# An attention stage: the scaling of the probabilities moved from VectorE to ScalarE

## The chip, the cores and the metric

The kernel runs on one core of a Trainium2 chip. Its engines work side by side, each through its own queue of instructions in order: TensorE (PE in the profile; its weight loads are PEld) multiplies matrices into PSUM, VectorE (DVE) and ScalarE (ACT) compute elementwise, GpSimd (POOL) and SyncE (SP) here mainly start DMAs. An instruction starts when its engine has come to it and the semaphores it waits for have been raised. The metric is the time of one execution on the device in microseconds (us), lower being better.

## What is computed

One decoder layer on 512 tokens with 2048 features: RMSNorm, a token mixer, a SwiGLU feed-forward part, and a last RMSNorm. The mixer is an attention of 16 heads (128 wide, 4 heads to a group of keys and values) with three branches, whose outputs are added with gates:

```python
gates = jax.nn.sigmoid(gl)                       # per token, branch and head
p_c = masked_softmax(s_c, mask_c)                # 31 compressed blocks of keys
o_c = jnp.einsum('bghtc,bcgd->btghd', p_c, vcc)
...                                              # o_s: selected blocks; o_w: sliding window
o = gates[0] * o_c + gates[1] * o_s + gates[2] * o_w
return o.reshape(Bsz, S, N_HEADS * DH) @ w_out
```

With 512 tokens all 8 blocks are selected and the window holds every earlier token, so the selected and the window branch are each a full causal attention, with keys and values of their own. A masked softmax divides exponentials by their row sum. The kernel therefore multiplies each row of exponentials by one factor, gate over sum, and then adds the branches up in one accumulation.

## The kernel before

All products are made in float32 from two parts: a high part rounded for TensorE, and the rest that the rounding leaves (names ending in h and l, or `whi`, `wlo`). Splitting a tile takes a copy on ScalarE (L97, L866, L293) and a subtraction on VectorE (L98, L870, L294), and a product takes three matmuls (L268 to L270).

The attention stage is a loop over heads `h` (L906), here called rounds 0 to 15, each of 12 steps `i`. In round `h` the values of head `h` are multiplied while head `h+1` gets its scores; both are cut into tiles of 128 tokens, `t` for queries (3 first, 0 last) and `kt` for keys. Between these pieces `pump` (L773) lets the stream `dense` put out the projections of later heads' queries, keys and values and, from round 12 on, part of the output projection: 20.8 us of TensorE work to a round by its own count. The order on every engine is the order of this Python code. A tile of probabilities goes this way:

- `scores(h+1, t)` at steps 2, 5, 8, 11 (t = 3, 2, 1, 0): score matmuls into the one PSUM tile `s`; VectorE adds the bias and takes the row maxima (`mx`, L828) for three regions: the 31 compressed columns (`cx`) and two branches of 128(t+1) columns each; ScalarE takes the exponentials and row sums (`sm`, L830) into `CX[t]` and `P[t]`.
- `finish(h+1, t)` at the next step (3, 6, 9, and step 0 of the following round for t = 0): VectorE takes the reciprocal of the sums (L835), multiplies it by the gates (L836), scales the three pieces (L842; the compressed one is copied three times into `P[t]`, 96 columns), and turns `P[t]` in blocks of 32x32 (L843); four DMAs on SyncE's queue store it to DRAM (L845).
- `fetch(t)` (L849) brings it back as `ptr`, so that keys lie on the partitions: tiles 3 and 2 at step 8, 1 at step 11, 0 at step 2 of the following round.
- `turn(h, b, kt)` at steps 0 to 8 splits it for branch `b` into `pth` (ScalarE, L866) and `ptl` (VectorE, L870), three and two buffers; `values` multiplies it two steps later into PSUM tile `o` (L884). `head_out` copies `o` to `stage` after step 11 (L890).

Within a step the order is `turn`, then `scores` or `finish`, then `values`, then `pump`. Ahead of round 0 the first head's four tiles go through `scores`, `finish` and `fetch` without rounds (L899 to L905). Weight tiles (`raw`, three buffers, loaded by GpSimd's queue in this stage) are split two granules ahead of their use.

Of the kernel before, what the change touches and what calls it, by code (L numbers as in the profile page):

```python
# [13 lines left out]
AF = mybir.ActivationFunctionType  # L14
OP = mybir.AluOpType
# [4 lines left out]
S, D, H, DH, G, HPG = 512, 2048, 16, 128, 4, 4  # L20
# [153 lines left out]
def nsa_block(ctx: ExitStack, tc: tile.TileContext, x, rel_bias, mix_g, ffn_g, fin_g, w_in, w_out,  # L174
              pos_k, w1k, w2k, pos_v, w1v, w2v, f_in, f_out, onehot, out):
    nc = tc.nc
    mm, act, dve, pool = nc.tensor.matmul, nc.scalar.activation, nc.vector, nc.gpsimd
# [28 lines left out]
    def tok(t):  # L206
        return slice(128 * t, 128 * (t + 1))
# [59 lines left out]
    def three(o, ah, al, bh, bl, start, stop):  # L267
        mm(o, ah, bh, start=start, stop=False, skip_group_check=True)  # L268
        mm(o, ah, bl, start=False, stop=False, skip_group_check=True)  # L269
        mm(o, al, bh, start=False, stop=stop, skip_group_check=True)  # L270
# [80 lines left out]
    with ExitStack() as st1:  # L351
# [11 lines left out]
        with ExitStack() as st0:  # L363
# [35 lines left out]
            def bank(shape):  # L399
                return ps1.tile(shape, F32, name=next(names))  # L400
# [49 lines left out]
            p = bank([128, 512])  # L450
            for i in range(N_WARM):
                nc.tensor.transpose(p[:, 128 * (i % 4):128 * (i % 4 + 1)], ident, ident)
            p = bank([128, KC])
# [29 lines left out]
            for q in range(4):  # L483
# [23 lines left out]
                if q == 3:  # L507
                    p = bank([128, S])
# [100 lines left out]
        for i in range(8):  # L609
            g = W.take()  # L610
            for t in range(NT):
# [4 lines left out]
                if i == 7:  # L616
                    act(ge[:, t], ps[t][:, 256:304].rearrange("p (n h) -> p n h", n=3), AF.Exp,
                        scale=yneg[:, t:t + 1])
                    v_out(ps[t][:, :256], t, VV[0][0][:, t], VV[0][1][:, t])
            if i == 1:  # L620
                p = ps1.tile([128, 128], F32, name="tr")
# [27 lines left out]
        p = ps1.tile([96, G, 128], F32, name="tr")  # L649
# [8 lines left out]
    with ExitStack() as st2:  # L658
# [3 lines left out]
        runs = [32 * (2 * t + 3) for t in range(NT)]  # L662
        P = [ap_.tile([128, 4, runs[t]], F32, name=f"p{t}", bufs=1) for t in range(NT)]
        CX = [ap_.tile([128, 32], F32, name=f"cx{t}", bufs=1) for t in range(NT)]
# [108 lines left out]
        def pump(h, step):  # L773
            at = h + (step + 4) / STEPS
            goal = 20800 * min(at, 13) + 22500 * max(at - 13, 0)
            while done["ns"] < goal:
                c = next(stream, "end")
                if c == "end":
                    return
                done["ns"] += c or 0  # L780

        def drain_to(n):
            while done["n"] < n:
                c = next(stream, "end")
                if c == "end":
                    return
                done["ns"] += c or 0

        def needed(h):

            return 4 * ((h - 2) // 4) + (1 if h % 4 > 1 else 3) if h > 1 else 0

        TB, HS = {}, {}
        sc = ps2.tile([128, 3, 512], F32, name="s", bufs=1).rearrange("p a c -> p (a c)")

        def load_bias(h):
            if h < H:
                TB[h] = ap_.tile([128, S], F32, name="tb")
                (nc.sync if h else pool).dma_start(TB[h], bass.AP(tensor=d_u.tensor, offset=d_u.offset + h * UL + 127,
                                                 ap=[[H * UL - 1, 128], [1, S]]))  # L800

        def branch(t, b):

            return P[t][:, :, 32 * (t + 1) * b:32 * (t + 1) * (b + 1)]

        def scores(h, t):
            g, n = h // HPG, 128 * (t + 1)
            (qh, ql), (kh, kl) = Q[h], KK[g % 2]
            if t == NT - 1:
                HS[h] = dict(  # L810
                    mx=ap_.tile([128, NT, 3], F32, name="mx"), sm=ap_.tile([128, NT, 3], F32, name="sm"))
            s = HS[h]
            at = 224 + (512 if t == 1 else 0)
            cuts = [0, 288] + [c for c in (800, 1056) if c <= 32 + 2 * n]
            if cuts[-1] < 32 + 2 * n:
                cuts.append(32 + 2 * n)
            for c0, c1 in zip(cuts, cuts[1:]):
                three(sc[:, at + c0:at + c1], qh[:, tok(t)], ql[:, tok(t)], kh[:, c0:c1], kl[:, c0:c1], True, True)
            c = CX[t][:, :NCMP]
            regions = [(c, c, c, sc[:, at:at + NCMP], biasc[:, h, 24 - 8 * t:24 - 8 * t + NCMP])]  # L820
            bt = TB[h][:, S - n:].rearrange("p (n s) -> p n s", s=128)
            sw = sc[:, at + 32:at + 32 + 2 * n].rearrange("p (n b s) -> p b n s", b=2, s=128)
            for b in range(2):
                u = ap_.tile([128, S], F32, name="u")[:, :n]
                regions.append((u.rearrange("p (n s) -> p n s", s=128), u.rearrange("p (n j s) -> p j n s", j=4, s=32),
                                branch(t, b).rearrange("p j (n s) -> p j n s", s=32), sw[:, b], bt))
            for i, (u, v, p, ps, bias) in enumerate(regions):
                dve.tensor_tensor_reduce(out=u, in0=ps, in1=bias, op0=OP.add, op1=OP.min, scale=-1.0,  # L828
                                         scalar=1e38, accum_out=s["mx"][:, t, i:i + 1])
                act(p, v, AF.Exp, bias=s["mx"][:, t, i:i + 1], scale=-1.0, accum_out=s["sm"][:, t, i:i + 1])  # L830
            s[t] = [c] + [branch(t, b) for b in range(2)]

        def finish(h, t):
            r = HS[h]["sm"][:, t]
            dve.reciprocal(r, r)  # L835
            dve.tensor_mul(r, r, gates[:, t, h])  # L836
            for i, p in enumerate(HS[h].pop(t)):
                o = p
                if not i:
                    o = P[t][:, :3, runs[t] - 32:]  # L840
                    p = CX[t].unsqueeze(1).to_broadcast([128, 3, 32])
                dve.tensor_scalar(o, p, r[:, i:i + 1], None, op0=OP.mult)  # L842
            dve.transpose(P[t], P[t])  # L843
            for i in range(4):
                nc.sync.dma_start(d_p[t][:, :, i].rearrange("j a r -> a j r"), P[t][32 * i:32 * (i + 1)])  # L845

        def fetch(t, queue=nc.sync):

            queue.dma_start(PT[:, :, PT_STEP * t:PT_STEP * t + runs[t]], d_p[t].rearrange("j a i r -> (j a) i r"))  # L849
# [6 lines left out]
        def turn(h, b, kt):  # L856
            n = S - 128 * kt
            th = ap_.tile([128, 512], F32R, name="pth", bufs=3)
            tl = ap_.tile([128, 512], F32R, name="ptl") if b >= 0 else th
            rows = 128 if b >= 0 else 96  # L860
            if b < 0:
                src = arrived(rows, 64, 0, PT_STEP + 64)
            else:
                src = arrived(rows, PT_STEP * kt + 32 * (kt + 1) * b + 32 * kt, kt, PT_STEP + 32 * b)
            th4, tl4 = (x[:rows, :n].rearrange("p (t i s) -> p t i s", i=4, s=32) for x in (th, tl))
            act(th4, src, AF.Copy)  # L866
            if b < 0:
                dve.tensor_tensor(th4[32:64], src[32:64], th4[32:64].bitcast(F32), op=OP.subtract)
            else:
                dve.tensor_tensor(tl4, src, th4.bitcast(F32), op=OP.subtract)  # L870
            HS[h]["t", b, kt] = th[:rows, :n], tl[:rows, :n]
# [27 lines left out]
        for i in range(4):  # L899
            scores(0, 3 - i)  # L900
            if i > 1:
                fetch(5 - i, pool)
            if i:
                finish(0, 4 - i)
            pump(-1, min(9 + i, 11.7))  # L905
        for h in range(H):  # L906
            seq = [(b, kt) for kt in (3, 2, 1, 0) for b in (0, 1)] + [(-1, 0)]
            for i in range(STEPS):
                if i == 4:
                    load_bias(h + 2)  # L910
                if i == 2:
                    fetch(0, nc.sync if h else pool)
                if i < 9:
                    turn(h, *seq[i])
                if i == 8 and h + 1 < H:
                    fetch(3)
                    fetch(2)
                if i == 11 and h + 1 < H:
                    fetch(1)
                if i == 0:  # L920
                    if not h:
                        fetch(1, pool)
                    finish(h, 0)
                if h + 1 < H:
                    if i == 2:
                        drain_to(needed(h + 1))
                    if i % 3 == 2:
                        scores(h + 1, 3 - i // 3)
                    elif i % 3 == 0 and i:
                        finish(h + 1, 4 - i // 3)  # L930
                if 2 <= i < 10 or i == 11:
                    if i == 2 and h % HPG == 0:
                        drain_to(h)
                    values(h, *seq[min(i - 2, 8)])
                    if i == 11:
                        head_out(h)
                pump(h, i)
# [563 lines left out]
    c = slice(1536, 2048)  # L1501
# [46 lines left out]
```

## Time and profile before

| what | value |
|---|---|
| median of three timed runs | 2126.79 us (2126.36 to 2128.25) |
| profiled execution, first to last instruction (span) | 2124.1 us |
| busy: TensorE, VectorE, ScalarE, GpSimd | 2100.1, 1634.4, 932.7, 125.8 us |
| attention stage in the trace | about 200 to 697 us |
| mean granted clock of TensorE | 0.996 |

The page gives no other time for the profiled execution than its span; what lies ahead of the first and behind the last instruction is in the timed runs only, whose median is 2.7 us longer. A timeline row gives the start and the length in us, the engine, the line, the instruction, what it writes and reads with the shape, a count, and in brackets how long the engine had been idle and what ended that. A row of the groups gives the count, then busy us and mean ns of one, then idle us ahead of them and what ended it. A row of the waits gives who waited for whom: us in total, times, the longest. A row of the stretches gives for each engine busy us and, as x, instructions, then TensorE's granted clock, the DMA share and GB/s.

### The profile page before, as it was taken

The numbers are of one execution on the slowest core, as the hardware profiler recorded it, in microseconds if no ns is written. First come the engines' busy times: TensorE is split into PE (matmuls) and PEld (weight loads), VectorE is DVE, ScalarE is ACT, GpSimd is POOL, SyncE is SP. The second block draws the span as 40 slices with busy tenths as digits, with TensorE's granted clock in tenths as the row PEclk, the third lists the DMA queues.
The fourth block names the chain that finished last, engine by engine and source line by source line (L and its number), as shares of the span: only waits on it lengthen the run. The fifth ranks groups of instructions, "written<-read, shape, count | busy, mean of one in ns | idle before, by whom it ended". The sixth has DMA issues, their size and how long they took to land.

```text
span 2124.1 us, 37169 instructions
## 1 busy us (share of the span) xinstructions
PE 2100.1 (99%) x14693; PEld 1948.4 (92%) x14693; DVE 1634.4 (77%) x2671; ACT 932.7 (44%) x1448; POOL 125.8 (6%) x206
## 2 busy tenths in 40 slices
PE   9999999999999999999999999999999999999998
PEld 7898788888989889999999999999999888999996
DVE  5565777877786366898888888888888777877785
ACT  5344455455554334444334343443434444444344
POOL 1000111111111000000000000000000000001000
PEclk9999999999999999999999999999999999999999
DMA  7555666676676643344344333433333776878894
GB/s 230 173 157 151 193 192 201 183 199 189 194 236 199 246 141 109 126 135 128 120 130 130 120 128 122 130 126 124 122 124 124 272 273 214 303 269 311 308 335 144
DMA packets 273227, 388.08 MB, mean 183 GB/s; under 512 B 34235, under 2 KB 205819, under 8 KB 272412
## 3 DMA queue, kind: packets, MB, share of 16 engines
q1 hardware_dynamic: 248252, 279.71, 41.7%
q0 software_dynamic: 22896, 102.31, 14.0%
q10 hardware_dynamic: 1904, 3.68, 0.5%
q8 instruction: 115, 1.88, 0.4%
q14 instruction: 60, 0.49, 0.1%
HBM read 320.52 MB, written 70.36 MB: 184 GB/s over the span
## 4 chain that ended last, share of the span: by engine, by line
PE 69%; DVE 0%; DMA 0%; ACT 0%; issue 0%; ACTq 0%
PE f L269 19%; PE f L268 19%; PE f L270 19%; PE proj L268 2%; PE proj L269 2%; PE proj L270 2%; PE pp L268 1%; PE pp L270 1%; PE pp L269 1%; PE po L269 1%; PE po L268 1%; PE po L270 1%; PE pp L246 0%; DMA acc<-d_a 0%; PE o L269 0%; PE o L270 0%
## 5 line engine op out<-in xcount | busy, mean ns | idle before, releaser
L98 DVE TENSOR_TENSOR wlo<-raw,whi 128x1024 fp32r<-128x1024 f32 (+1 forms) x225 | 269.4, 1199 | 117.6 <-ACT whi L97 117.3
L97 ACT ACTIVATE whi<-raw 128x1024 fp32r<-128x1024 f32 (+1 forms) x225 | 233.3, 1040 | 221.6 <-DVE raw L1038 122.9
L1038 DVE TENSOR_TENSOR tlo<-tt,thi 128x1536 fp32r<-128x1536 f32 (+2 forms) x135 | 197.1, 1460 | 111.0 <-ACT thi L1143 86.7
L269 PE MATMUL f<-hn_l,whi 128*128 128x256 f32 x984 | 271.6, 276 | 0.0
L270 PE MATMUL f<-hn_h,wlo 128*128 128x256 f32 x984 | 271.6, 276 | 0.0
L268 PE MATMUL f<-hn_h,whi 128*128 128x256 f32 x984 | 271.6, 276 | 0.0
L1138 ACT ACTIVATE whi<-raw 128x1024 fp32r<-128x1024 f32 x123 | 126.1, 1057 | 293.6 <-DVE raw L1038 290.2
L268 PE MATMUL proj<-hn_h,whi 128*128 128x512 f32 x512 | 204.8, 400 | 0.7 <-ACT hn_h L410 0.7
L269 PE MATMUL proj<-hn_l,whi 128*128 128x512 f32 x512 | 201.0, 393 | 0.3 <-DVE hn_l L411 0.3
L270 PE MATMUL proj<-hn_h,wlo 128*128 128x512 f32 x512 | 200.9, 392 | 0.0
L269 PEld LDWEIGHTS f<-hn_l,whi 128*128 128x128 f32 x984 | 184.7, 188 | 0.0
L268 PEld LDWEIGHTS f<-hn_h,whi 128*128 128x128 f32 x984 | 184.7, 188 | 0.0
L270 PEld LDWEIGHTS f<-hn_h,wlo 128*128 128x128 f32 x984 | 184.7, 188 | 0.0
L1143 ACT ACTIVATE thi<-tt 128x1536 fp32r<-128x1536 f32 x82 | 121.9, 1486 | 82.3 <-PE f L269 70.6
L270 PE MATMUL proj<-whi,hn_l 128*128 128x256 f32 (+2 forms) x496 | 146.1, 295 | 2.9 <-DVE hn_l L731 2.9
L1038 DVE TENSOR_TENSOR wlo<-raw,whi 128x1024 fp32r<-128x1024 f32 x123 | 147.0, 1223 | 1.1 <-ACT whi L1138 1.1
L268 PE MATMUL proj<-whi,hn_h 128*128 128x256 f32 (+2 forms) x496 | 146.5, 295 | 0.8 <-ACT hn_h L730 0.8
L269 PE MATMUL proj<-wlo,hn_h 128*128 128x256 f32 (+2 forms) x496 | 145.5, 293 | 0.0
L270 PE MATMUL f<-whi,tlo 128*128 128x512 f32 x320 | 124.9, 390 | 0.2 <-DVE tlo L1038 0.2
L269 PE MATMUL f<-wlo,thi 128*128 128x512 f32 x320 | 124.9, 390 | 0.0
L268 PE MATMUL f<-whi,thi 128*128 128x512 f32 x320 | 124.7, 390 | 0.0
L270 PEld LDWEIGHTS proj<-hn_h,wlo 128*128 128x128 f32 x512 | 96.7, 189 | 21.7 <-DVE wlo L98 0.2
(329 smaller groups left out, 6104.3 us busy)
## 6 DMA issues: line engine op xcount, KB each, us to landing
raw<-in_ffn_w_in SPq DMA_DIRECT2D x135, 512.0 KB, 3.6
raw<-in_ffn_w_out SPq DMA_DIRECT2D x88, 512.0 KB, 5.8
rawx<-in_ffn_w_in SPq DMA_DIRECT2D x41, 512.0 KB, 4.8
rawx<-d_a SPq DMA_DIRECT2D x31, 512.0 KB, 5.1
ah<-d_s POOLq DMA_DIRECT2D x16, 896.0 KB, 7.3
al<-d_s POOLq DMA_DIRECT2D x16, 896.0 KB, 9.4
raw<-in_nsa_w_in POOLq DMA_DIRECT2D x24, 512.0 KB, 4.7
raw<-in_nsa_w_in SPq DMA_DIRECT2D x23, 512.0 KB, 5.3
```

Source lines behind the costliest of these rows:

```text
L97: self.nc.scalar.activation(hi[:, :n], src, AF.Copy)
L98: self.nc.vector.tensor_tensor(lo[:, :n], src, hi[:, :n].bitcast(F32), op=OP.subtract)
L268: mm(o, ah, bh, start=start, stop=False, skip_group_check=True)
L269: mm(o, ah, bl, start=False, stop=False, skip_group_check=True)
L270: mm(o, al, bh, start=False, stop=stop, skip_group_check=True)
L1038: dve.tensor_tensor(o, a, b, op=OP.subtract)
L1138: act(h, r, AF.Copy)
L1143: act(h, ttf, AF.Copy)
```

## The change

`finish` becomes two functions. `weigh` makes the factors on VectorE as before and does the three multiplications on ScalarE, the two branches first, then the compressed columns; `send` turns the tile and stores it. In a step `weigh` now stands ahead of `turn`, `send` where `finish` stood. `scores` no longer keeps a list of pieces. From here on line numbers behind L838 are one higher.

```diff
-            s[t] = [c] + [branch(t, b) for b in range(2)]
-
-        def finish(h, t):
+
+        def weigh(h, t):
+
             r = HS[h]["sm"][:, t]
             dve.reciprocal(r, r)
             dve.tensor_mul(r, r, gates[:, t, h])
-            for i, p in enumerate(HS[h].pop(t)):
-                o = p
-                if not i:
-                    o = P[t][:, :3, runs[t] - 32:]
-                    p = CX[t].unsqueeze(1).to_broadcast([128, 3, 32])
-                dve.tensor_scalar(o, p, r[:, i:i + 1], None, op0=OP.mult)
+            for b in range(2):
+                p = branch(t, b)
+                act(p, p, AF.Copy, scale=r[:, b + 1:b + 2])
+            c = CX[t].unsqueeze(1).to_broadcast([128, 3, 32])
+            act(P[t][:, :3, runs[t] - 32:], c, AF.Copy, scale=r[:, :1])
+
+        def send(h, t):
             dve.transpose(P[t], P[t])
...
             if i:
-                finish(0, 4 - i)
+                weigh(0, 4 - i)
+                send(0, 4 - i)
...
+                if not i:
+                    weigh(h, 0)
+                elif i % 3 == 0 and h + 1 < H:
+                    weigh(h + 1, 4 - i // 3)
                 if i < 9:
                     turn(h, *seq[i])
...
-                    finish(h, 0)
+                    send(h, 0)
...
-                        finish(h + 1, 4 - i // 3)
+                        send(h + 1, 4 - i // 3)
```

What that does to the queues: the names `p_1857`, `p_1856`, `p_1855`, `p_1854` are `P[3]` to `P[0]`, and `cx_1861` to `cx_1858` are `CX[3]` to `CX[0]`. On ScalarE, from the end of one round (`stage`) to step 3 of the next, before:

```order
L890 ACTIVATE stage<-o 128x512
L866 ACTIVATE pth<-ptr 128x128
L97 ACTIVATE whi<-raw 128x1024
L866 ACTIVATE pth<-ptr 128x128
L866 ACTIVATE pth<-ptr 128x256
L830 ACTIVATE cx_1861,sm<-cx_1861,mx 128x31
L830 ACTIVATE p_1857,sm<-u,mx 128x4x128 x2
L866 ACTIVATE pth<-ptr 128x256
L97 ACTIVATE whi<-raw 128x1024
```

and now:

```order
L891 ACTIVATE stage<-o 128x512
L839 ACTIVATE p_1854<-p_1854,sm 128x4x32 x2
L841 ACTIVATE p_1854<-cx_1858,sm 128x3x32
L867 ACTIVATE pth<-ptr 128x128
L97 ACTIVATE whi<-raw 128x1024
L867 ACTIVATE pth<-ptr 128x128
L867 ACTIVATE pth<-ptr 128x256
L830 ACTIVATE cx_1861,sm<-cx_1861,mx 128x31
L830 ACTIVATE p_1857,sm<-u,mx 128x4x128 x2
L839 ACTIVATE p_1857<-p_1857,sm 128x4x128 x2
L841 ACTIVATE p_1857<-cx_1861,sm 128x3x32
L867 ACTIVATE pth<-ptr 128x256
```

The three multiplications of tile 0 now stand ahead of step 0's split and weight split, and those of tile 3 between step 2's exponentials and step 3's split. On VectorE at step 3, between the maxima of step 2 and those of step 5:

```order
-L870 TENSOR_TENSOR ptl<-ptr,pth 128x256
-L835 RECIPROCAL sm<-sm 128x3
-L836 TENSOR_TENSOR sm<-sm,gates 128x3
-L842 TENSOR_SCALAR p_1857<-cx_1861,sm 128x3x32
-L842 TENSOR_SCALAR p_1857<-p_1857,sm 128x4x128 x2
-L843 STREAM_TRANSPOSE p_1857<-p_1857 128x1152
-L98 TENSOR_TENSOR wlo<-raw,whi 128x1024
-L870 TENSOR_TENSOR ptl<-ptr,pth 128x384 x2
+L835 RECIPROCAL sm<-sm 128x3
+L836 TENSOR_TENSOR sm<-sm,gates 128x3
+L871 TENSOR_TENSOR ptl<-ptr,pth 128x256
+L844 STREAM_TRANSPOSE p_1857<-p_1857 128x1152
```

The two small operations on the factors come ahead of the split's rest (`ptl`) instead of behind it, and the multiplications are gone from between them and the transpose. At step 9 there is no `turn`, and VectorE goes from the factors straight to the transpose and then to step 11's maxima:

```order
 L835 RECIPROCAL sm<-sm 128x3
 L836 TENSOR_TENSOR sm<-sm,gates 128x3
-L842 TENSOR_SCALAR p_1855<-cx_1859,sm 128x3x32
-L842 TENSOR_SCALAR p_1855<-p_1855,sm 128x4x64 x2
-L843 STREAM_TRANSPOSE p_1855<-p_1855 128x640
+L844 STREAM_TRANSPOSE p_1855<-p_1855 128x640
 L828 ISA cx_1858,mx<-s,biasc 128x31
```

Only the multiplications left this queue there. TensorE's and SyncE's rows stand in the same order as before.

## Prediction

> **What bounds the kernel now.** I read the page's engine table first, then the stretches of the attention stage, then who waits for whom there, then the timeline of one head.
>
> ```profile
> PE 2100.1 (99%) x14693; PEld 1948.4 (92%) x14693; DVE 1634.4 (77%) x2671; ACT 932.7 (44%) x1448; POOL 125.8 (6%) x206
> ```
>
> ```profile
> core 0: us, PE busy (x) PEld busy (x) DVE busy (x) ACT busy (x) POOL busy (x), PEclk, DMA share, GB/s
> 200.00:245.00 45.00, 40.58 (x185) 33.62 (x184) 33.64 (x96) 20.11 (x55) 7.53 (x10) 0.92 0.61 170
> 245.00:700.00 455.00, 449.71 (x2735) 401.46 (x2734) 345.88 (x947) 235.44 (x612) 62.52 (x84) 1.00 0.69 200
> ```
>
> TensorE is busy for 99% of the span, and in the stage that the change touches (200 to 700 us) it is idle for 4.4 + 5.3 us. So hardly anything is left to win. What counts is what could make TensorE wait, and that shows in the waits of the other two engines in the same stage (total us, times, longest):
>
> ```profile
> ACT cx L830 <- DVE mx L828: 158.7, 64, 4.1
> DVE ptl L870 <- ACT pth L866: 63.3, 44, 2.9
> DVE cx L828 <- PE s L270: 2.1, 2, 1.6
> ```
>
> VectorE waits 63.3 us for ScalarE's split of the fetched probabilities, ScalarE waits 158.7 us for VectorE's row maxima, and VectorE waits for TensorE's scores only twice. So the two run as one chain, handing work to and fro, and that chain does not wait for TensorE: it is late against it all the time. How late, the timeline shows in head 6's round, first VectorE, then TensorE:
>
> ```profile
> 424.87 0.08 DVE L828 DVE_READ_ACCUMULATOR2_ANT mx<- 128x1 f32 x1
> ```
>
> ```profile
> 424.69 0.28 PE L269 MATMUL proj<-wlo,hn_h 128*128 128x256 f32 x1
> 424.81 0.28 PE L270 MATMUL proj<-whi,hn_l 128*128 128x256 f32 x1
> 425.01 0.40 PE L268 MATMUL s<-k1h,qh 128*128 128x288 f32 x1
> ```
>
> The score matmul of step 11 overwrites PSUM that VectorE has read until 424.95, and it starts at 425.01, where the rhythm of the matmuls ahead (0.12 us apart) would have had it at 424.93. So in this round TensorE arrives just when the chain lets it: the chain's round is as long as TensorE's, and the slack is gone. Whatever lengthens the chain from here on lengthens the stage; whatever shortens it gains almost nothing.
>
> **The change, part by part.** Off VectorE go 192 multiplications; onto ScalarE come 192. Rows of the groups kept apart by shape (mean ns of one):
>
> ```profile
> L842 DVE TENSOR_SCALAR p<-cx,sm 128x96 f32<-128x96 f32 x64 | 18.4, 288 | 2.5
> L842 DVE TENSOR_SCALAR p<-p,sm 128x512 f32<-128x512 f32 x32 | 14.2, 487 | 0.0
> L842 DVE TENSOR_SCALAR p<-p,sm 128x384 f32<-128x384 f32 x32 | 11.7, 409 | 0.0
> L842 DVE TENSOR_SCALAR p<-p,sm 128x256 f32<-128x256 f32 x32 | 9.8, 347 | 0.0
> L830 ACT ACTIVATE p<-u,mx 128x512 f32<-128x512 f32 x32 | 22.9, 716 | 3.3 <-DVE mx L828 3.0 <-ACT cx L830 0.2
> L830 ACT ACTIVATE p<-u,mx 128x384 f32<-128x384 f32 x32 | 19.5, 610 | 1.1
> L830 ACT ACTIVATE p<-u,mx 128x256 f32<-128x256 f32 x32 | 16.0, 502 | 0.0
> L830 ACT ACTIVATE p<-u,mx 128x128 f32<-128x128 f32 x32 | 12.4, 387 | 0.0
> L830 ACT ACTIVATE cx<-cx,mx 128x31 f32<-128x31 f32 x64 | 20.6, 321 | 158.7 <-DVE mx L828 158.7
> L866 ACT ACTIVATE pth<-ptr 128x512 fp32r<-128x512 f32 x32 | 19.5, 616 | 0.7 <-DMA ptr<-d_p 0.7
> ```
>
> ScalarE's multiplication is not in this trace. The nearest row is the exponential, which also takes a per-row operand from SBUF: 716, 610, 502, 387 ns. The lower end is the split without such an operand (616 ns for 512, so 0.1 less each). The 96-column copy lies between 321 (31 columns) and 387 (128): an estimate of 360. I take the exponential's row, because its operands are of the same kind. Following instructions overlap by about 0.1 us (below: 0.71 long, the next starts 0.61 later), so they advance by 0.61, 0.51, 0.40, 0.29 and 0.27; the upper end is no overlap.
>
> The Trainium skill (Perfetto Trace Analysis, Optimizing Scalar/DVE Operations) says that VectorE is faster where a 2x mode is available, and that moving work to ScalarE may make sense where VectorE is saturated. The trace agrees with the first (487 against 716 ns); on the second VectorE is busy 0.76 of the stage, so by that rule the move would win nothing, and the sum below says that it costs.
>
> The sum hangs on the handover. Step 3 of the round, VectorE and ScalarE:
>
> ```profile
> 405.93 0.08 DVE L828 DVE_READ_ACCUMULATOR2_ANT mx<- 128x1 f32 x1
> 407.30 0.42 DVE L870 TENSOR_TENSOR ptl<-ptr,pth 128x256 fp32r<-128x256 f32 x1 [1.28 <-ACT pth L866]
> 407.64 0.17 DVE L835 RECIPROCAL sm<-sm 128x3 f32<-128x3 f32 x1
> 408.04 0.29 DVE L842 TENSOR_SCALAR p<-cx,sm 128x96 f32<-128x96 f32 x1
> 408.24 0.87 DVE L842 TENSOR_SCALAR p<-p,sm 128x512 f32<-128x512 f32 x2
> 409.14 1.38 DVE L843 STREAM_TRANSPOSE p<-p 128x1152 f32<-128x1152 f32 x1
> ```
>
> ```profile
> 406.16 0.71 ACT L830 ACTIVATE p<-u,mx 128x512 f32<-128x512 f32 x1
> 406.77 0.19 ACT L830 ACTIVATION_READ_ACCUMULATOR p<-u,mx 128x1 f32 x1
> 406.86 0.40 ACT L866 ACTIVATE pth<-ptr 128x256 fp32r<-128x256 f32 x1
> ```
>
> Now: the split on ScalarE starts at 406.86, VectorE takes its rest at 407.30, then reciprocal and product (0.40), three multiplications (1.10, to 409.14), transpose. Afterwards the split stands behind the three multiplications, and these behind the factors, which need the last row sum (406.96). So ahead of the split come 0.10 (to 406.96), 0.04 to VectorE (407.26 to 407.30 is such a handover), 0.36 for the two small operations, 0.05 back, and 2 x 0.61 + 0.27 = 1.49 on ScalarE: 2.04. Behind it 0.40 + 1.10 = 1.50 fall away. Net **+0.54 us**. Nothing hides it: VectorE's next instructions (the split's rest, the transpose, the next weight split) are queued in order behind it, and it would wait there anyway.
>
> Step 6 (384 columns) alike: 2 x 0.51 + 0.27 + 0.55 = 1.84 ahead, and behind it 0.40 + 0.95 less (the multiplications 0.29 + 2 x 0.41, less 0.16, as 0.29 + 2 x 0.49 took 1.10 in step 3): **+0.49**. Step 9 (256) has no split in between: 2 x 0.40 + 0.36 + two handovers of 0.04 = 1.24 in place of 0.29 + 2 x 0.35 - 0.16 = 0.83: **+0.41**. In step 0 something covers it:
>
> ```profile
> 400.33 0.58 ACT L890 ACTIVATE stage<-o 128x512 f32<-128x512 f32 x1
> 401.00 1.05 ACT L97 ACTIVATE whi<-raw 128x1024 fp32r<-128x1024 f32 x1
> ```
>
> ```profile
> 402.96 1.18 DVE L98 TENSOR_TENSOR wlo<-raw,whi 128x1024 fp32r<-128x1024 f32 x1
> ```
>
> The three small multiplications (2 x 0.29 + 0.27 = 0.85, and some 0.06 of waiting for the factors, an estimate from the handovers of step 3) put the weight split's end from 402.05 to 402.96, and VectorE gets to that split's rest at 402.96 today, having done its own multiplications: **+0.05**. Without this cover it would be 0.9. Together the chain's round grows by 0.54 + 0.49 + 0.41 + 0.05 = **1.5 us**. Bounds: 0.1 us less in each of the nine multiplications of steps 3, 6 and 9 (no cost for the operand) gives 0.6, and 0.1 more (no overlap) gives 2.4.
>
> The start, before any round, is a run of such handovers (ScalarE, VectorE, TensorE):
>
> ```profile
> 209.04 0.19 ACT L830 ACTIVATION_READ_ACCUMULATOR p<-u,mx 128x1 f32 x1
> ```
>
> ```profile
> 209.72 1.38 DVE L843 STREAM_TRANSPOSE p<-p 128x1152 f32<-128x1152 f32 x1
> ```
>
> ```profile
> 220.92 0.45 PE L268 MATMUL o<-pth,v0h 128*128 128x128 f32 x1 [2.80 <-issue]
> ```
>
> The first transpose must now wait for ScalarE's exponentials of the second tile (to 209.23) and 1.49 of multiplications: 210.76 instead of 209.72, +1.0. The second tile adds 0.9 more in the same way, and its way through DRAM brings that to the chain: **+1.9** (0.9 to 2.8 by the same bounds).
>
> The new first half issues no DMA; the transpose's four stores and the fetches keep their places in SyncE's queue and move with the chain. GpSimd's weight loads wait for VectorE's weight splits and move with it too; two granules are held ready, so TensorE does not meet that. TensorE's own order is unchanged.
>
> How long does this last? Rounds 0 to 11 and the first half of round 12; after that the weight work thins out and TensorE is no longer met. At the meeting point of round 12 (VectorE, then TensorE):
>
> ```profile
> 607.12 0.08 DVE L828 DVE_READ_ACCUMULATOR2_ANT mx<- 128x1 f32 x1
> ```
>
> ```profile
> 607.80 0.29 PE L268 MATMUL s<-k1h,qh 128*128 128x288 f32 x1
> ```
>
> Slack there is 607.80 - 607.20 = 0.6. So: 1.9 + 12 x 1.5 + 1.0 (steps 3 and 6) - 0.6 = **+20.3 us**. Bounds: 0.9 + 12 x 0.6 + 0.4 - 0.6 = 8, and 2.8 + 12 x 2.4 + 1.6 - 0.6 = 32.6. The span of 2124.1 would be 2144.4. The median of the runs, 2126.79, lies 2.7 above the profiled span, and I leave that as it is: **2147 us**, from 2135 to 2159.
>
> **The rivals.** *Hidden* (8%): TensorE stays the bound and VectorE's spare time swallows the handovers: 2127. For it speaks TensorE's 99%, against it the 0.06 us of slack at 425.01 and that VectorE waits for ScalarE, not for TensorE. [...]
>
> *Faster* (5%): what limits the chain is VectorE's own work, and ScalarE's multiplications fit into its idle time, as if the 1.28 us of waiting took them in. Then a round of the chain loses some 3.5 us (1.10 + 0.95 + 0.83 and the small tile's), TensorE never waits in the rounds, and at most the 5.3 us of idle time between 245 and 700 come back: 2121.5. It would need the multiplications to run beside the split instead of ahead of it; the order on ScalarE says ahead.
>
> *Much slower* (7%): TensorE's new waits also drop its clock.
>
> ```profile
> 218.00:221.00 3.00, 0.20 (x3) 0.11 (x1) 0.15 (x1) 0.49 (x2) 2.27 (x3) 0.91 1.01 303
> 221.00:227.00 6.00, 6.00 (x17) 5.01 (x18) 3.56 (x15) 2.29 (x9) 0.76 (x1) 0.50 0.76 237
> ```
>
> After a wait of 2.80 us the granted clock was 0.50 for 6 us, so about 3 us of work were lost. Twelve times that on top: 2147 + 36 = 2183. It decides from waits of nearly 3 us in one piece; I expect some 1.5 per round. The Trainium skill (TensorE: Matmul & The Clock Gate, What's actually happening) halves the clock after an idle window of about 3.4 us; this trace agrees with the half, and shows it after 2.8.
>
> **How the numbers follow.** The forecast with its bounds has 80%, so the range is theirs, 2135 to 2159. Two kernels can be told apart here by about 0.2%, 4.3 us. The forecast and *much slower* lie above that: slower 87%. *Hidden* is the same, 8%. *Faster* 5%.
>
> **What would show it.** In the changed kernel's profile the ScalarE multiplications should have means of about 716, 610, 502 and 387 ns, and 360 for the copies; VectorE should wait for ScalarE's scaled tiles ahead of its transposes or split rests; TensorE's score matmul of step 11 should wait for the maxima in most rounds, and a round from score to score should last about 31.4 us. I am wrong if TensorE's idle time between 200 and 700 us stays near 10 us, and in the size if the scaling comes out nearer to 616 than to 716 ns.

## The result, and the profile after

| | median | lowest to highest | profiled span |
|---|---|---|---|
| before | 2126.74 us | 2126.36 to 2128.25 | 2124.1 us |
| after | 2151.22 us | 2150.24 to 2154.0 | 2148.8 us |

The changed kernel is slower, by 24.5 us going by the two medians. The ratio of the runs is 1.0122 (95%: 1.011 to 1.0135), which is clear of 1 and would be 25.9 us. The forecast was 20.3 us more, 2147 us, with a range of 2135 to 2159. Below, a difference in us of a timed kernel is its ratio's share of the kernel before that ran beside it (2125.8 and 2125.5 us in the experiments).

The page's engine table of the changed kernel:

```profile
PE 2114.3 (98%) x14693; PEld 1948.9 (91%) x14693; DVE 1580.4 (74%) x2479; ACT 1012.4 (47%) x1640; POOL 125.8 (6%) x206
```

VectorE has 54 us of work less, ScalarE 80 us more, and neither has become a full engine. TensorE's busy time grew by 14.2 us with the same 14693 matmuls, so the rise is best read as waiting that is shown as longer matmuls (the 16 matmuls 128x512 of `ptl` with `v1h` have a mean of 438 ns where they had 410). The weight loads' busy time, 1948.9 against 1948.4 us, shows that the work is the same. The Trainium skill (Perfetto Trace Analysis, Identifying the Most-Contended Engine) says that the busy share of the matmuls is not a good measure of how close TensorE is to its peak, and names the busy share of the weight loads among what to use instead; this trace agrees, the first rose by 14.2 us while the kernel became slower, the second by 0.5.

The stretches of the attention stage, which now ends some 25 us later:

```profile
core 0: us, PE busy (x) PEld busy (x) DVE busy (x) ACT busy (x) POOL busy (x), PEclk, DMA share, GB/s
200.00:245.00 45.00, 38.10 (x170) 30.77 (x169) 24.11 (x69) 25.00 (x68) 6.73 (x9) 0.92 0.55 150
245.00:720.00 475.00, 460.13 (x2723) 399.74 (x2721) 297.61 (x776) 306.40 (x783) 62.51 (x84) 1.00 0.67 190
```

TensorE is idle for 6.9 + 14.9 us where it had been idle for 4.4 + 5.3. The granted clock is 0.92 and 1.00, as before. Who waits for whom there (200 to 722 us; total us, times, longest):

```profile
ACT cx L830 <- DVE mx L828: 97.6, 64, 2.4
DVE ptl L871 <- ACT pth L867: 88.4, 49, 4.6
DVE sm L835 <- ACT p L830: 39.6, 44, 1.0
ACT p L839 <- DVE sm L836: 37.1, 48, 1.8
DVE p L844 <- ACT p L841: 25.2, 18, 2.2
```

The last two are new: ScalarE waits 48 times for the factors, VectorE waits 18 times for scaled tiles ahead of the transpose. VectorE's wait for ScalarE's split grew from 63.3 to 88.4 us, and its wait for the row sums, ahead of the factors, from 2.5 us (3 times) to 39.6. These two and the wait ahead of the transpose together grew by 87 us. What reaches TensorE is seen best at its weight loads, which show more of it than the matmuls (22.3 us against 8.1 in the change, for VectorE's split rests). Before (200 to 697 us), then after:

```profile
PEld s L268 <- DVE mx L828: 4.0, 7, 1.3
PEld o L269 <- DVE ptl L870: 3.0, 5, 1.0
```

```profile
PEld o L269 <- DVE ptl L871: 22.3, 43, 1.5
PEld s L268 <- DVE mx L828: 9.7, 14, 2.2
```

These two waits together are 25.0 us longer. Most of it is met not at the score matmul, as I had expected, but at the matmuls that use VectorE's rest of the split. In one round of the changed kernel (weight loads, in brackets the wait):

```profile
393.46 0.19 PEld L269 LDWEIGHTS o<-ptl,v1h 128*128 128x128 f32 x1 [0.76 <-DVE ptl L871]
401.73 0.19 PEld L269 LDWEIGHTS o<-ptl,v1h 128*128 128x128 f32 x1 [0.41 <-DVE ptl L871]
406.84 0.19 PEld L268 LDWEIGHTS s<-k1h,qh 128*128 128x128 f32 x1 [0.70 <-DVE mx L828]
416.68 0.19 PEld L269 LDWEIGHTS o<-ptl,v1h 128*128 128x128 f32 x1 [0.40 <-DVE ptl L871]
```

So TensorE is held four times in this round, 2.3 us in all, three times by split rests. The same four places recur in the other steady rounds, with waits of 0.15 to 0.76 us; the scores of step 11 start 0.05 to 0.06 us behind the maxima in each of rounds 0 to 11, and between 300 and 600 us their weight loads wait 0.31 to 0.72 us.

**The terms of the sum.** The start of VectorE's first row-maximum instruction (`cx<-s`) of each tile marks the chain's round: tile 3 at step 2, then tiles 2, 1, 0 and the next round's tile 3. Before, then after:

```profile
374.72 0.19 DVE L828 CUSTOM_DVE_ANT_0 cx<-s,biasc 128x31 f32<-128x31 f32 x1
382.62 0.18 DVE L828 CUSTOM_DVE_ANT_0 cx<-s,biasc 128x31 f32<-128x31 f32 x1
394.19 0.19 DVE L828 CUSTOM_DVE_ANT_0 cx<-s,biasc 128x31 f32<-128x31 f32 x1
399.04 0.15 DVE L828 CUSTOM_DVE_ANT_0 cx<-s,biasc 128x31 f32<-128x31 f32 x1
404.60 0.18 DVE L828 CUSTOM_DVE_ANT_0 cx<-s,biasc 128x31 f32<-128x31 f32 x1
```

```profile
385.32 0.18 DVE L828 CUSTOM_DVE_ANT_0 cx<-s,biasc 128x31 f32<-128x31 f32 x1
393.79 0.18 DVE L828 CUSTOM_DVE_ANT_0 cx<-s,biasc 128x31 f32<-128x31 f32 x1
405.90 0.19 DVE L828 CUSTOM_DVE_ANT_0 cx<-s,biasc 128x31 f32<-128x31 f32 x1
411.17 0.15 DVE L828 CUSTOM_DVE_ANT_0 cx<-s,biasc 128x31 f32<-128x31 f32 x1
416.88 0.18 DVE L828 CUSTOM_DVE_ANT_0 cx<-s,biasc 128x31 f32<-128x31 f32 x1
```

The four intervals hold the handovers of steps 3, 6, 9 and 0:

| interval with | before | after | longer by | forecast |
|---|---|---|---|---|
| step 3 | 7.90 | 8.47 | 0.57 | 0.54 |
| step 6 | 11.57 | 12.11 | 0.54 | 0.49 |
| step 9 | 4.85 | 5.27 | 0.42 | 0.41 |
| step 0 | 5.56 | 5.71 | 0.15 | 0.05 |
| round | 29.88 | 31.56 | 1.68 | 1.5 |

Step 3 of the changed kernel a round later, VectorE and then ScalarE, shows where these come from:

```profile
419.27 0.18 DVE L835 RECIPROCAL sm<-sm 128x3 f32<-128x3 f32 x1 [0.98 <-ACT p L830]
419.48 0.16 DVE L836 TENSOR_TENSOR sm<-sm,gates 128x3 f32<-128x3 f32 x1
421.68 0.43 DVE L871 TENSOR_TENSOR ptl<-ptr,pth 128x256 fp32r<-128x256 f32 x1 [2.04 <-ACT pth L867]
422.02 1.37 DVE L844 STREAM_TRANSPOSE p<-p 128x1152 f32<-128x1152 f32 x1
```

```profile
419.05 0.19 ACT L830 ACTIVATION_READ_ACCUMULATOR p<-u,mx 128x1 f32 x1
419.74 1.34 ACT L839 ACTIVATE p<-p,sm 128x512 f32<-128x512 f32 x2 [0.50 <-DVE sm L836]
420.98 0.36 ACT L841 ACTIVATE p<-cx,sm 128x96 f32<-128x96 f32 x1
421.25 0.40 ACT L867 ACTIVATE pth<-ptr 128x256 fp32r<-128x256 f32 x1
```

The row sum is there at 419.24, VectorE takes it at 419.27 (0.03 us), has the factors at 419.64, ScalarE starts on them at 419.74 (0.10 us), needs 1.51 us to the split at 421.25, and VectorE stands still for 2.04 us. That is the path of the forecast instruction by instruction; the largest difference is the way from VectorE to ScalarE, 0.10 where 0.05 had been put.

### The profile page after: what moved, and what is told of

Same layout as the page of the kernel before. It is cut to its first block, busy times and chain, and to the rows that moved or that the text cites. A ratio compares the mean times of both kernels' runs of the same rounds, so it can differ in the third digit from the quotient of the medians.

```text
span 2148.8 us, 37125 instructions
## 1 busy us (share of the span) xinstructions
PE 2114.3 (98%) x14693; PEld 1948.9 (91%) x14693; DVE 1580.4 (74%) x2479; ACT 1012.4 (47%) x1640; POOL 125.8 (6%) x206
## 4 chain that ended last, share of the span: by engine, by line
PE 80%; ACT 7%; DVE 7%; issue 3%; DMA 2%; SPq 0%; ACTq 0%; DVEq 0%; POOL 0%; POOLq 0%
PE f L268 19%; PE f L269 19%; PE f L270 19%; PE proj L268 5%; PE proj L269 5%; PE proj L270 5%; DVE wlo L98 2%; ACT p L830 2%; ACT p L839 1%; ACT whi L97 1%; DVE ptl L871 1%; PE pp L268 1%; PE pp L270 1%; PE pp L269 1%; PE po L268 1%
## 5 line engine op out<-in xcount | busy, mean ns | idle before, releaser
L871 DVE TENSOR_TENSOR ptl<-ptr,pth 128x128 fp32r<-128x128 f32 (+3 forms) x128 | 60.0, 486 | 90.8 <-ACT pth L867 88.4
```

## The experiments

The theory: what costs is the place of the multiplications, in a path of handovers ahead of the split, and each 0.1 us on that path is paid once a round because TensorE has no slack. The rivals: ScalarE's added load as such; and, for the parts, that step 0 isn't covered, that the start costs more, or that the late rounds cost nothing. Each edit is against the changed kernel.

To split each time into its parts, the three stretches of the stage were read from each trace: from TensorE's first score matmul of head 0 to the first `cx<-s` of round 0 (the start), from there to that of round 12 (twelve rounds), and from there to the start of TensorE's last three score matmuls (the late rounds).

| kernel | start | 12 rounds | late rounds | against before |
|---|---|---|---|---|
| before | 23.56 | 359.91 | 91.89 | |
| the change | 27.26 | 378.59 | 95.28 | +3.7, +18.7, +3.4 |
| order alone (VectorE) | 23.67 | 355.89 | 91.09 | +0.1, -4.0, -0.8 |
| ScalarE behind the split | 27.21 | 356.13 | 93.02 | +3.7, -3.8, +1.1 |
| shared | 23.56 | 355.12 | 90.83 | 0, -4.8, -1.1 |
| one copy more | 27.49 | 398.41 | 97.56 | +3.9, +38.5, +5.7 |
| heads 13 to 15 only | 23.58 | 359.27 | 95.37 | 0, -0.6, +3.5 |
| head 0 only | 27.02 | 359.23 | 91.89 | +3.5, -0.7, 0 |
| tile 3 only | 24.50 | 366.16 | 93.29 | +0.9, +6.3, +1.4 |
| tile 0 only | 23.23 | 360.51 | 92.80 | -0.3, +0.6, +0.9 |

In the change's trace, for example, the two `cx<-s` that mark the middle column start at 227.58 and 606.17: 606.17 - 227.58 = 378.59. (Before's twelve rounds hold a few longer ones, so their mean is 29.99 and not the steady 29.88.)

**Order alone: all of it on VectorE, but ahead of the split.**

```diff
-            for b in range(2):
-                p = branch(t, b)
-                act(p, p, AF.Copy, scale=r[:, b + 1:b + 2])
             c = CX[t].unsqueeze(1).to_broadcast([128, 3, 32])
-            act(P[t][:, :3, runs[t] - 32:], c, AF.Copy, scale=r[:, :1])
+            dve.tensor_scalar(P[t][:, :3, runs[t] - 32:], c, r[:, :1], None, op0=OP.mult)
+            for b in range(2):
+                p = branch(t, b)
+                dve.tensor_scalar(p, p, r[:, b + 1:b + 2], None, op0=OP.mult)
```

> The new order with the old engine: the factors and all three multiplications stand ahead of the split, but VectorE does the multiplications. In series (my theory: the chain of VectorE and ScalarE sets the rounds, each operation in its path counts one for one): the multiplications now fill VectorE's wait for the split. From the rows of before, the transpose comes earlier by 0.3 us in step 3 (408.84 for 409.14), 0.5 in step 6, 0.7 in step 0, the same in step 9: 1.5 us less in a round, so the chain falls below TensorE's own round of about 29.7 us and only some 3 to 5 us can be won: 2122 to 2125 us. Rival, the order costs: if what made the change slow is that the split stands behind the scaling, most of the loss stays: 2140 to 2151 us. Rival, ScalarE's load: as before, 2127 us.

Measured: 2120.39 us, ratio 0.9975 (0.9966 to 0.9984), faster than before, and some 2 us below the expected times. Its VectorE at step 3:

```profile
404.30 0.16 DVE L835 TENSOR_TENSOR sm<-sm,gates 128x3 f32<-128x3 f32 x1
404.50 0.28 DVE L837 TENSOR_SCALAR p<-cx,sm 128x96 f32<-128x96 f32 x1
404.70 0.87 DVE L840 TENSOR_SCALAR p<-p,sm 128x512 f32<-128x512 f32 x2
405.49 0.41 DVE L870 TENSOR_TENSOR ptl<-ptr,pth 128x256 fp32r<-128x256 f32 x1
405.82 1.37 DVE L843 STREAM_TRANSPOSE p<-p 128x1152 f32<-128x1152 f32 x1
```

The split's rest at 405.49 has no wait in brackets: ScalarE splits while VectorE multiplies. From the factors' end (404.46) to the transpose it is 1.36 us, against 2.38 in the change. From round 1 on the rounds are 29.69 to 29.87 us, 29.76 on average. No row of TensorE waits in them (250 to 570 us), and the first maxima of tile 3 follow 0.61 us behind the end of its scores, in before 1.0 to 2.4 in rounds 1 to 11: the chain now waits for TensorE. That is why 1 us less in this step does not bring 12 us.

**The same ScalarE work, behind the split.** `weigh` keeps the factors; the three multiplications go into a function that `send` calls first.

```diff
         def weigh(h, t):
             r = HS[h]["sm"][:, t]
             dve.reciprocal(r, r)
             dve.tensor_mul(r, r, gates[:, t, h])
+
+        def scale(h, t):
+            r = HS[h]["sm"][:, t]
             for b in range(2):
...
         def send(h, t):
+            scale(h, t)
             dve.transpose(P[t], P[t])
```

> ScalarE does all three multiplications as in the change, the factors stand early, but the multiplications stand behind the split on ScalarE instead of ahead of it. ScalarE has the same instructions as in the change. In series: the transpose against before comes 0.1 us earlier in step 3, 0.7 earlier in step 6, 0.4 later in step 9, and the weight split of step 0 up to 0.15 later: 0.2 us less in a round, and the start costs about 1.5, so 2124 to 2131 us. Rival, ScalarE's load: the 80 us that ScalarE has more to do are what delays the splits, wherever they stand: 2145 to 2152 us, as in the change. Rival, the price of the handover alone (two crossings per tile): the handovers stay, about half the loss stays, 2138 us.

Measured: 2126.3 us, ratio 1.0004 (0.9994 to 1.0013). ScalarE's busy time is the change's (1011.7 against 1012.4 us), and the 24.5 us are gone. ScalarE's load is thereby refuted as the cause, and so is a price of the crossings alone, which are all still there (2138 us was expected for it); what is left is the place. Its ScalarE at step 3:

```profile
408.36 0.40 ACT L870 ACTIVATE pth<-ptr 128x256 fp32r<-128x256 f32 x1
408.95 1.34 ACT L841 ACTIVATE p<-p,sm 128x512 f32<-128x512 f32 x2 [0.19 <-DVE sm L835]
```

The split at 408.36 goes first, so VectorE's factors and split rest lie beside ScalarE's. The twelve rounds are 3.8 us shorter than before, the late ones 1.1 longer, and the start gives 3.7 back: ahead of round 0 there is no `turn` between `weigh` and `send`, so that its order is the change's.

**Shared: ScalarE one branch behind its split, VectorE the other two pieces ahead of it.**

```diff
-            for b in range(2):
-                p = branch(t, b)
-                act(p, p, AF.Copy, scale=r[:, b + 1:b + 2])
             c = CX[t].unsqueeze(1).to_broadcast([128, 3, 32])
-            act(P[t][:, :3, runs[t] - 32:], c, AF.Copy, scale=r[:, :1])
+            dve.tensor_scalar(P[t][:, :3, runs[t] - 32:], c, r[:, :1], None, op0=OP.mult)
+            p = branch(t, 1)
+            dve.tensor_scalar(p, p, r[:, 2:3], None, op0=OP.mult)
+
+        def scale(h, t):
+            p = branch(t, 0)
+            act(p, p, AF.Copy, scale=HS[h]["sm"][:, t][:, 1:2])
 
         def send(h, t):
+            scale(h, t)
             dve.transpose(P[t], P[t])
```

> VectorE scales the compressed columns and the second branch ahead of the split, ScalarE scales the first branch behind its split, at the same time. In series: against before the transpose comes 0.75 us earlier in step 3, 0.9 in step 6, 0.3 in step 9, 0.6 in step 0: 2.5 us less in a round, below TensorE's own round, so TensorE bounds: 2121 to 2125 us, hardly better than with all of it on VectorE in the new order. ScalarE's load: a third of the load, a third of the loss, about 2134 us.

Measured: 2119.66 us, ratio 0.9972 (0.9962 to 0.9982), the lowest median of all, 1.3 us below the expected times, and by the intervals the same as order alone. Once the chain is shorter than TensorE's round, shortening it further buys nothing that these runs tell apart.

**One copy more: the change, with the compressed columns scaled twice to the same place.**

```diff
-            act(P[t][:, :3, runs[t] - 32:], c, AF.Copy, scale=r[:, :1])
+            for _ in range(2):
+                act(P[t][:, :3, runs[t] - 32:], c, AF.Copy, scale=r[:, :1])
```

> The change with the scaling of the compressed columns done twice (0.36 us, 0.27 in sequence, 64 more instructions, 17 us of advance on ScalarE in all). In series: 0.27 us more in steps 3, 6 and 9 and in step 0, where the cover is used up: 1.1 us per round, 12.5 rounds, and 0.8 at the start: 13 to 15 us over the change, 2164 to 2166 us. Rival, TensorE or another bound has taken over in the changed kernel: less than 5 us more, under 2156 us.

Measured: 2176.45 us, ratio 1.0238 (1.0224 to 1.0252), 25 us above the change, not 13 to 15. The size was missed because of the price of the second copy, not of the number of times that it is paid. ScalarE at step 3:

```profile
433.21 0.77 ACT L842 ACTIVATE p<-cx,sm 128x96 f32<-128x96 f32 x2
433.88 0.40 ACT L868 ACTIVATE pth<-ptr 128x256 fp32r<-128x256 f32 x1
```

From the first copy to the split there are 0.67 us where one copy took 0.27, so the copy that was added cost 0.40. Four times that is 1.6 a round, and twelve rounds grew by 398.41 - 378.59 = 19.8 us, 1.65 each. So what is added to this path comes back in the round to within 0.05 us. It comes back in all four steps (0.40 or 0.41 in each interval), step 0 included, which the weight split no longer covers here.

**Which heads and tiles pay.** Four kernels make the change for some heads or tiles only, the others scale in `send` on VectorE as before:

```diff
+        def moved(h, t):
+            return h >= 13      # or: h == 0; t == 3; t == 0
+
         def weigh(h, t):
+            if not moved(h, t):
+                return
...
         def send(h, t):
+            if not moved(h, t):
+                r = HS[h]["sm"][:, t]
+                dve.reciprocal(r, r)
+                dve.tensor_mul(r, r, gates[:, t, h])
+                c = CX[t].unsqueeze(1).to_broadcast([128, 3, 32])
+                dve.tensor_scalar(P[t][:, :3, runs[t] - 32:], c, r[:, :1], None, op0=OP.mult)
+                for b in range(2):
+                    p = branch(t, b)
+                    dve.tensor_scalar(p, p, r[:, b + 1:b + 2], None, op0=OP.mult)
             dve.transpose(P[t], P[t])
```

Heads 13 to 15 only:

> The change for heads 13 to 15 only (rounds 12 to 14), the others as before. The prediction gave these rounds 1.0 us and nothing after round 12. In series: the score matmuls of the changed kernel lie 20.8 us behind those of before at the start of round 12 and 25.0 at the start of round 14, so the late rounds cost more than I counted, about 4 us: 2129.5 to 2131 us. Rival, the late rounds cost nothing of their own and only pass on what the earlier ones lost: 2126 to 2127 us.

Measured: 2129.35 us, ratio 1.0019 (1.001 to 1.0028), +4.0 us, just under the expected times. That the late rounds cost nothing is refuted. Two of TensorE's rows of waits between 575 and 705 us, whose longest (1.1 us each) the change has too:

```profile
PE o L268 <- ACT pth L880: 2.7, 3, 1.1
PE o L269 <- DVE ptl L884: 2.4, 4, 1.1
```

Head 0 only:

> The change for the four tiles of head 0 only. In series: the chain starts 1.9 us later, and as its round before is as long as TensorE's it never makes that up: about 1.5 to 2 us, 2127.5 to 2128 us. Rival, a delay at the start is absorbed in the rounds that follow: 2126 us.

Measured: 2127.74 us, ratio 1.001 (1.0001 to 1.0018), +2.1 us. That is the expected time, but not by the expected amounts: at the first maxima its chain is 3.5 us late, not 1.9, and at the last scores 2.8, so part of it is made up on the way.

Tile 3 only:

> The change for query tile 3 only (step 3 of each round), in all heads. In series: 0.6 us in each of 12 rounds, 1.0 at the start, about 1 in the late rounds, less a slack below 0.6: 8.5 to 9.5 us, 2134 to 2136 us. Rival, the steps don't add up, because a chain relieved in steps 6, 9 and 0 makes up for step 3: 2126 to 2129 us.

Measured: 2134.96 us, ratio 1.0039 (1.0026 to 1.0053), +8.3 us, as expected. A steady round of its chain lasts from the `cx<-s` at 377.73 to that at 408.20: 408.20 - 377.73 = 30.47, 0.59 more than before's 29.88, all in the interval of step 3, which was priced at 0.54.

Tile 0 only:

> The change for query tile 0 only (step 0 of each round), in all heads. In series: the weight split that follows on ScalarE covers it, so 0.05 (the prediction) to 0.15 us (steps of the changed kernel) in each of 13 rounds: 0.5 to 2 us, 2126.5 to 2128 us. Rival, nothing is covered: 0.9 us in each round, 11 to 12 us, 2138 us.

Measured: 2127.12 us, ratio 1.0006 (0.9997 to 1.0015), not clear of zero. An uncovered 0.9 us a round would have made 2138. In the rounds the weight split does cover step 0 all but for the 0.15 us that the change has there too (the interval is 5.71 us, 5.57 before).

## Why the prediction was nearly right, and where it failed

**The mechanism holds.** Two engines that are not full, but hand work to each other in a chain, set the round, and TensorE's 99% did not protect it. *Hidden* (2127) is refuted by the result, and *Faster* (2121.5) too: VectorE's 54 us of saved work did not shorten the chain. The kernel with order alone shows what it did lack: it comes out at 2120.39 with not one instruction moved off VectorE, because the multiplications then lie beside ScalarE's split. *Much slower* (2183) failed at its own condition: the waits came in pieces of at most 0.8 us in the steady rounds, and the granted clock between 245 and 720 us stayed at 1.00.

**The price of ScalarE's multiplications** was right:

```profile
L839 ACT ACTIVATE p<-p,sm 128x512 f32<-128x512 f32 x32 | 21.4, 715 | 8.6 <-DVE sm L836 8.6
L841 ACT ACTIVATE p<-cx,sm 128x96 f32<-128x96 f32 x64 | 23.0, 359 | 0.0
```

715 and 359 ns, against 716 and 360 in the forecast; for 384, 256 and 128 columns it was 609, 502 and 395, against 610, 502 and 387.

**The round** was 1.68 us longer, not 1.5. Half of the difference lies in steps 3, 6 and 9, which together are 0.09 us longer than forecast (0.03, 0.05 and 0.01), and half in step 0, 0.15 in place of 0.05. The mis-sized term is the handover from VectorE to ScalarE, which all four have: 0.10 us where 0.04 to 0.05 had been taken from a handover in the other direction. In step 9 nearly all of it was made up elsewhere. In step 0 ScalarE waits 0.11 us longer ahead of the multiplications, where 0.06 was put, and the rest of the weight split takes 1.22 us for 1.18. Counted over the twelve rounds that is 18.7 us against 18.0, since the profiled kernel before had some rounds longer than its steady ones. The slack of 0.06 us was read from one round: in the kernel before, the scores of step 11 start 0.06 us behind the maxima in five of the twelve rounds and 0.13 to 0.79 us behind them in the others. That changed little, as the chain's round, 31.56 us, then exceeded TensorE's by more than 1 us.

**The start** was +3.7 us at the first maxima, not +1.9. With head 0 alone it is 3.5 there and 2.8 at the end of the stage, and 2.1 (0.2 to 3.8) in the timed runs. The excess is not in the handovers between VectorE and ScalarE: tile 2's transpose, then the split of step 2 that reads it, before and after:

```profile
213.17 1.11 DVE L843 STREAM_TRANSPOSE p<-p 128x896 f32<-128x896 f32 x1
223.88 0.42 ACT L866 ACTIVATE pth<-ptr 128x256 fp32r<-128x256 f32 x1 [2.86 <-DMA ptr<-d_p]
```

```profile
214.29 1.11 DVE L844 STREAM_TRANSPOSE p<-p 128x896 f32<-128x896 f32 x1 [1.86 <-ACT p L841]
226.79 0.42 ACT L867 ACTIVATE pth<-ptr 128x256 fp32r<-128x256 f32 x1 [4.92 <-DMA ptr<-d_p]
```

Counted from the first score matmul (201.11 and 200.32), the transpose is 1.91 us later, as forecast, and the split 3.70. Between them lies the way through DRAM, which the prediction took to be as long as before. The four stores of tile 2 (112 KB each) took 4.9 us from issue to landing where they had taken 2.1, and GpSimd's fetch of the tile, which waits for them, was issued at 222.60 instead of 218.73; the fetch itself was 0.9 us shorter. The stores follow the transpose, and the fetch of tile 3 was issued 0.46 us behind that transpose's end, where it had been 1.38. The four kernels in which ScalarE does all the scaling of head 0 have such slow stores (4.4 to 4.9 us), the other six have 2.1. That the stores and the fetch of tile 3 got in each other's way is a reading of this and was not tried.

**The step that failed** is "after that the weight work thins out and TensorE is no longer met". It gave 1.0 - 0.6 = 0.4 us to everything from round 12 on; the trace has 3.4, and heads 13 to 15 alone have 3.5. The sum had priced the new waits of VectorE for ScalarE, and left out the reverse one: ScalarE's multiplications, and the split queued behind them, wait for VectorE to come to the factors. At step 0 of round 13 VectorE is held by other splits at just that moment. The change at step 0 of round 13, VectorE, ScalarE, TensorE:

```profile
639.61 1.23 DVE L98 TENSOR_TENSOR wlo<-raw,whi 128x1024 fp32r<-128x1024 f32 x1 [0.26 <-ACT whi L97]
640.75 1.22 DVE L731 TENSOR_TENSOR hn_l<-hn_l,hn_h 128x1024 fp32r<-128x1024 f32 x1
641.89 0.17 DVE L835 RECIPROCAL sm<-sm 128x3 f32<-128x3 f32 x1
```

```profile
642.35 0.69 ACT L839 ACTIVATE p<-p,sm 128x128 f32<-128x128 f32 x2 [1.83 <-DVE sm L836]
643.22 0.49 ACT L867 ACTIVATE pth<-ptr 128x128 fp32r<-128x128 f32 x2
```

```profile
643.56 0.33 PE L268 MATMUL o<-pth,v1h 128*128 128x128 f32 x1 [1.10 <-ACT pth L867]
```

ScalarE stands still for 1.83 us behind two splits of VectorE that have nothing to do with the tile, then multiplies, and TensorE waits 1.10 us for the split. In the kernel before, this split (617.09 on ScalarE) followed its predecessor at once, since nothing ahead of it needed VectorE. With tile 0 alone the same wait appears at the same place (0.97 us), and the late rounds grow by 0.9. That accounts for about 0.9 of the 3.4 us. How the other 2.5 us divide among the tiles and the output projection's splits was read only in part and stays open: tile 3 alone has 1.4.

**The sum.** 3.7 + 18.7 + 3.4 = 25.8, less 0.8 because the stage began 0.8 us earlier in this profile than in that of before, less 0.3 behind the last scores: 24.7, the difference of the spans. The forecast had 1.9 + 18.0 + 0.4. It came out within the range since its bounds were those of ScalarE's price, which was hit; that the start and the late rounds, together 4.8 us above the forecast, fitted in too was luck.

**What would show it** named the score matmul of step 11. It does wait in every steady round (0.31 to 0.72 us), but three of the four places are others, the matmuls that read VectorE's split rests. As the round is the chain's, the place where TensorE meets it changes nothing in the time.

## What to carry to other kernels

Where two engines hand work to and fro, as here, busy shares do not tell what a move between them costs: write down the path from one handover to the next, with what stands ahead of what in each queue, and look for the slack of the engine that it feeds. Work moved to an emptier engine adds its full length to the chain if it stands ahead of something that the other engine waits for (1.51 us in step 3, more than the 1.10 that VectorE had needed for it); with the same instructions behind it, or the old ones ahead of it, the same change was worth about 0 and -5 us here. A moved instruction also takes its inputs' queue along: ask what the giving engine is doing when the receiving one needs its operand, and what transfers a later result will run beside, in every phase of the loop and not only the steady one.

## What the runs showed of the hardware

- From the end of VectorE's factors to ScalarE's instruction that reads them it took 0.10 us (419.64 to 419.74; 0.09 or 0.10 in each of the 36 cases between 230 and 600 us in which ScalarE waited for them), from ScalarE's row sum to VectorE 0.03 us (419.24 to 419.27).
- Two ScalarE copies of 128x96 behind one another, with the same operands and the same place to write, took 0.67 us up to the next instruction, and one took 0.27: the second cost 0.40. Whether the place or the operands make the difference was not tried.
- ScalarE's multiplication by a per-row factor took the time of its exponential of the same shape (715 and 716 ns for 128x512, 502 and 502 for 128x256).
- The same four stores of 112 KB each took 2.1 us from issue to landing in six of the ten kernels and 4.4 to 4.9 in four (tile 2 of head 0, at the start of the stage).
